# The order of work in the merges and at the output of a hybrid flow-matching step

## The chip, the cores and the metric

One core of one Trainium2 chip runs the kernel. The metric is the device time of one execution in microseconds. Five instruction streams matter: TensorE (PE, with its weight loads listed apart as PEld), VectorE (DVE), ScalarE (ACT), GpSimd (POOL) and SyncE (SP), which here only issues DMAs. Each stream runs in the order in which it was laid down; an instruction that waits holds up all that stands behind it on the same engine.

## The reference, cut to what matters

One layer of a hybrid backbone runs on 2048 noisy tokens ("sample") and 128 context tokens ("prompt"), with a model width of 1024. Three branches of width 512 are computed from the same projection: a bidirectional chunked gated-delta scan, a spatial-gating MLP and a Fourier mix. What this change touches is behind the branches:

```python
    br = jnp.stack([o_a, o_b, o_c], axis=2)
    pb = jnp.einsum('btnw,nwd->btnd', br, w_branch)
    gt = jax.nn.sigmoid(gates.reshape(B, T, N_BRANCH, D_MODEL))
    merged = jnp.einsum('btnd,btnd->btd', gt, pb)
    return jnp.einsum('btd,de->bte', merged, w_out), s_f, s_b
...
    h = h + gate[:, None, :] * out
    y_sample = rmsnorm(h, final_g)
```

`rmsnorm` divides a row by the root of its mean square (plus 1e-6) and multiplies by `final_g`. The prompt gets the same end with its own gate. All data are float32.

## The kernel before, in words

**Numbers.** A float32 matrix is held as two float16 parts, hi and lo, and a product is three matmuls: hi by hi, hi by lo, lo by hi. Before a weight block is split, its squares are summed on ScalarE (L309, into `wss`, then cast as `wscb`), a small matmul with ones on TensorE spreads the sum, VectorE makes a power of two from it (L271 to L273), and ScalarE and VectorE write hi and lo (L321, L322). `weight_step` advances this by one step at a time, between tiles of other work.

**Merges.** `merge(n, ...)` runs once for each branch, in the order 1 (MLP), 2 (Fourier), 0 (scan). For each of 8 column blocks `db` and each of 5 token tiles (four of 512, one of 128) there is a gate product of 24 matmuls on `xh`, `xl`, a sigmoid on ScalarE (L1717, remembered in `gated_[0]`), a branch product of 12 matmuls on `o16` (`big`), a product with the gate on VectorE (L1723 or L1726), and for the later branches an addition on POOL (L1727). `o16` is filled by `branch_block`: it loads a row of the branch's output (`st<-br`), converts it to hi on ScalarE (L1683) and to lo on VectorE (L1684). The first merge converts two tiles ahead of its first gate and the others as it goes; in its last block it converts the rows of the next merge behind each tile, and so does the second merge for the third. While the first two merges run, the steps of the scan are laid in between by a pace-maker (`pace`); `pace.drain()` in the last block of the second merge ends the scan.

**Order.** The planner of the kernel's framework lays the instructions of each engine into a queue with a timeline model, in order of readiness and of the program. Some edges are written by hand: `tc.issue_after(x)` puts the instructions of a block behind `x` on the same engine, and `tc.high_priority()` puts them forward. `behind_gate()` gives the weight squares (L308) and the row conversions (L1682) such an edge to the newest gate, once there is one. `_InTurn` wraps VectorE, ScalarE and TensorE: while `kept` is true, each instruction gets an edge to the one before it, so that the queue is the program's order.

**Output.** The output product is computed for pairs of 128-token tiles by `two_tiles`, with seven products of 12 matmuls instead of eight, on operands `pa` that the last merge has prepared as sums and differences. Eight pairs run in the order of `firsts` (8, 10, 12, 14, 0, 2, 4, 6); `tw[0]` to `tw[3]` are sums of the output weights that all pairs use. Between products VectorE sums PSUM banks with SBUF (`total`, L2008), POOL multiplies by the gate and adds the residual rows (`gated`, L2003, L2004), and `rows_done` squares a row (L1972), takes the root on POOL (L254), scales on VectorE (L1974, with `fg`, which is final_g) and stores it. The last pair (`end`) is written out by hand: `gate_add` (two VectorE operations), `piece` (a square on ScalarE, and a product with `fg` in place on POOL or VectorE), `summed_up`, the roots on POOL (L2053), the scaling on ScalarE (L2054). The prompt's left half is done before the pairs (`prompt_left`), its right half behind them (`prompt_right`).

**Loads of the output.** `in_turn` issues loads on SP in a fixed order from `ahead_out`'s gate on: the prompt's left rows, `pa` of the first pair, `tw[1]`, the rows of the first pair, `tw[2]`, `tw[0]`, `tw[3]`, `fg`, the prompt's right gate and rows (`gp_right`, `x_right`), `pa` of the second pair, the rows of the second pair, `pa` of the third. Later pairs are loaded one by one as buffers come free; `pa` has three places: in the room of `xl`, in `opa` and in `orp`. `gp_right` is used first on POOL behind the fourth pair (L2126).

Of the kernel before, what the change touches and what calls it, by code (L numbers as in the profile page):

```python
# [14 lines left out]
AF = mybir.ActivationFunctionType  # L15
ALU = mybir.AluOpType
# [4 lines left out]
P = 128  # L21
D = 1024
# [166 lines left out]
def hybrid_flow_kernel(ctx: ExitStack, tc: tile.TileContext, x_prompt, x_sample, state_delta, c, c_ctx, w_ada,  # L189
# [45 lines left out]
    mhalf = sb(cp, [P, 1], "mhalf")  # L235
    G.memset(mhalf, -0.5)

    newest, gated_ = [None], [None]

    def behind_gate():  # L240
        return tc.issue_after(gated_[0].ins) if gated_[0] is not None else ExitStack()

    def mm(out, l, r, start=True, stop=True, reopened=False):
        newest[0] = PE.matmul(out, l, r, start=start, stop=stop, skip_group_check=reopened)  # L244
# [1531 lines left out]
    def finish_delta(db):  # L1776
        if db == KT - 1:
            pace.drain()

    early = list(range(KT))  # L1780

# [211 lines left out]
    def two_tiles(t, pa, xr, hh, end):  # L1993


        pl = ps_d if odd_pair[0] else ps_mm
        odd_pair[0] ^= 1
        a, Y, X = [bank(pl, [P, 512]) for _ in range(3)]
        p1 = sb(ep, [P, 512], "sg", bufs=4)
        u2, u3 = [sb(ep, [P, 512], "st", bufs=3) for _ in range(2)]  # L2000

        def gated(j, cs):
            G.tensor_tensor(hh[j][:, cs], hh[j][:, cs], gb[:, cs], ALU.mult)  # L2003
            G.tensor_tensor(hh[j][:, cs], hh[j][:, cs], xr[j][:, cs], ALU.add)  # L2004

        def total(out, ps, other):
            with tc.high_priority():
                V.tensor_tensor(out, ps, other, ALU.add)  # L2008
# [12 lines left out]
        product(X, pa, 3, summed(0), True)  # L2021
        total(hh[1][:, right], X, u3)
        if not end:
            gated(1, right)
            product(Y, pa, 2, summed(3), False)
            total(hh[1][:, left], Y, p1)
            gated(1, left)
            product(X, pa, 6, quarter(4, 512), False)
            total(hh[0][:, right], X, u2)
            gated(0, right)  # L2030
            for j in (1, 0):
                rows_done(t + j, hh[j], xr[j])
            return
        total(u2, X, u2)
        gate_add(p1, p1, gb[:, left], xr[1][:, left])
        gate_add(hh[1][:, right], hh[1][:, right], gb[:, right], xr[1][:, right])
        piece(1, 0, xr[1], hh[1], right, G)
        gate_add(u2, u2, gb[:, right], xr[0][:, right])
        piece(0, 0, xr[0], hh[0], left, G)
        product(Y, pa, 2, summed(3), False)  # L2040
        with tc.high_priority():
            gate_add(hh[1][:, left], Y, gb[:, left], p1)
            piece(1, 1, xr[1], hh[1], left, V)
        Z = bank(ps_mm, [P, 512])
        product(Z, pa, 6, quarter(4, 512), True)
        with tc.high_priority():
            made = gate_add(hh[0][:, right], Z, gb[:, right], u2)
            piece(0, 1, xr[0], hh[0], right, V)
        with tc.issue_after(made.ins):
            for j, i in ((1, 0), (0, 0), (1, 1), (0, 1)):  # L2050
                summed_up(j, i)
        for j in (1, 0):
            G.tensor_tensor(norms[:, j:j + 1], parts[j][:, 1:2], mhalf, ALU.pow)  # L2053
            A.activation(hh[j], hh[j], AF.Copy, scale=norms[:, j:j + 1])  # L2054
            SY.dma_start(y_sample[0, (t + j) * P:(t + j + 1) * P], hh[j])

    parts = [sb(op, [P, 3], f"part{j}", bufs=1) for j in range(3)]
    norms = sb(op, [P, 3], "norms", bufs=1)

    def piece(j, i, junk, h, cs, on):  # L2060
        squared = A.activation(junk[:, cs], h[:, cs], AF.Square, accum_out=parts[j][:, i:i + 1])
        if on is not None:
            on.tensor_tensor(h[:, cs], h[:, cs], fg[:, cs], ALU.mult)
        return squared

    def summed_up(j, i):
        q_ = parts[j]
        if i:
            V.scalar_tensor_tensor(q_[:, i:i + 1], q_[:, i:i + 1], 1.0 / D, q_[:, i - 1:i], ALU.mult, ALU.add)
        else:  # L2070
            V.tensor_scalar(q_[:, 0:1], q_[:, 0:1], 1.0 / D, EPS, ALU.mult, ALU.add)

    def gate_add(out, src, gate, other):
        V.tensor_tensor(out, src, gate, ALU.mult)
        return V.tensor_tensor(out, out, other, ALU.add)

    def prompt_left():
        ps = bank(ps_mm, [P, 512])
# [4 lines left out]
        A.activation(gp[0], x_left, AF.Square, accum_out=parts[2][:, 0:1])  # L2083

    def prompt_right():
        after = None
        for i, cs in ((1, slice(0, 384)), (2, slice(384, 512))):
            ps = bank(ps_mm, [P, cs.stop - cs.start])
            gemm_N(ps, *p16, wo, 512 + cs.start, cs.stop - cs.start)
            with tc.high_priority(), tc.issue_after(after.ins) if i > 1 else ExitStack():  # L2090
                after = gate_add(gp_right[:, cs], ps, gp_right[:, cs], x_right[:, cs])
                A.activation(x_right[:, cs], gp_right[:, cs], AF.Square, accum_out=parts[2][:, i:i + 1])
                (G if i == 1 else V).tensor_tensor(gp_right[:, cs], gp_right[:, cs], fg[:, 512 + cs.start:512 + cs.stop], ALU.mult)
        with tc.issue_after(after.ins):
            for i in range(3):
                summed_up(2, i)
        n_ = norms[:, 2:3]
        G.tensor_tensor(n_, parts[2][:, 2:3], mhalf, ALU.pow)
        A.activation(x_left, x_left, AF.Copy, scale=n_)
        A.dma_start(y_prompt[0, :, left], x_left)  # L2100
        V.tensor_scalar(gp_right, gp_right, n_, None, ALU.mult)
        SY.dma_start(y_prompt[0, :, right], gp_right)

    in_turn(x_left, xp_[0:P, left])
# [52 lines left out]
```

## Time and profile before

| | us |
|---|---|
| median of 3 runs | 2162.39 |
| lowest and highest | 2161.81, 2163.25 |
| the profiled execution, its own time | 2166.18 |
| span of its profile, first to last instruction | 2164.4 |

The profile is that of one execution. A view by stretches gives, for each stretch of the span, how long each engine was busy with how many instructions, the clock that was granted to TensorE (1.00 is full) and the busy share of the DMA engines. A row of a timeline gives the start, the length, the engine, the line, the operation, the tiles written and read (buffer numbers left out), and in brackets how long the engine stood idle before it and what ended that. In a table of waits the numbers are the sum, the count and the longest. A line can be that of a helper: all matmuls are L244, so the tile names tell them apart (`wohi`, `wolo`: output weights; `pa`: operands of a pair; `tw`: sums of weights; `xl`: the room in which some of these lie). SPq and ACTq rows are DMAs at the moment of their issue.

The stretches: the first merge begins near 1030, the second near 1390, the third near 1735; the output begins near 1993 with the prompt's left half, the last matmul ends near 2155, and the span ends at 2164.4.

### The profile page before, as it was taken

What the parts mean: (1) busy time and instruction counts of PE and PEld (TensorE: products, weight loads), DVE (VectorE), ACT (ScalarE), POOL (GpSimd) and SP (SyncE); (2) the same over time, 40 slices, a digit from 0 to 9 for tenths busy, and PEclk for the clock granted to TensorE, in tenths of its full rate; (3) what the DMA queues carried; (4) which work ended last, traced back from release to release, by engine and by line L of the source; (5) the groups of instructions that cost most, each with busy time, mean ns of one, the idle gap of its engine ahead of it and who ended that gap; (6) DMA issues with size and microseconds to landing.
All of it is one profiled execution on the core that took longest, in us unless ns stands there. A gap on an engine that the chain in (4) does not pass through costs nothing.

```text
span 2164.4 us, 42587 instructions
## 1 busy us (share of the span) xinstructions
PE 2088.8 (97%) x16133; PEld 1197.1 (55%) x16133; DVE 1357.1 (63%) x3101; ACT 1061.7 (49%) x2457; POOL 751.7 (35%) x933
## 2 busy tenths in 40 slices
PE   7999999999999999999899999999999999999998
PEld 4455444455555677777455555566555444444444
DVE  6656754389878797466655546756555554666245
ACT  5554744476555664445544445656543343453112
POOL 0321332233333432443222233345443234334364
PEclk9999999999999999999899999999999999999999
DMA  9525732277776743444655555867664645456852
GB/s 350 218 77 195 258 114 89 82 230 218 247 228 218 236 147 93 125 146 120 224 175 168 162 172 166 269 211 213 191 189 135 204 167 177 166 196 241 329 204 103
DMA packets 222909, 403.24 MB, mean 186 GB/s; under 512 B 39720, under 2 KB 109632, under 8 KB 219888
## 3 DMA queue, kind: packets, MB, share of 16 engines
q1 hardware_dynamic: 167664, 290.84, 42.2%
q0 software_dynamic: 15216, 65.89, 8.0%
q10 hardware_dynamic: 39824, 43.79, 6.1%
q8 instruction: 127, 2.08, 0.4%
q14 instruction: 78, 0.64, 0.1%
HBM read 258.19 MB, written 142.24 MB: 185 GB/s over the span
## 4 chain that ended last, share of the span: by engine, by line
PE 47%; DMA 8%; DVE 5%; ACT 2%; issue 1%; POOL 1%; SPq 0%; POOLq 0%; DVEq 0%; ACTq 0%
PE b L244 47%; DMA st<-br 2%; DMA pa<-pa 1%; DMA ES<-ei 1%; DMA br<-o 1%; DMA xh<-in_x_sample_dram 1%; DMA ei<-XB 1%; DVE big L1684 1%; DMA mrg<-mrow 0%; DMA S<-in_state_delta_dram 0%; DMA skn<-kv 0%; ACT big L1683 0%; PE b L1373 0%; DMA sn<-n 0%; DVE sg L470 0%
## 5 line engine op out<-in xcount | busy, mean ns | idle before, releaser
L244 PE MATMUL b<-xh,whi 128*128 128x512 f16 (+1 forms) x1920 | 650.9, 348 | 4.7 <-DVE sg L1447 2.5
L244 PE MATMUL b<-xl,whi 128*128 128x512 f16 (+1 forms) x1920 | 651.2, 348 | 0.0
L244 PE MATMUL b<-xh,wlo 128*128 128x512 f16 (+1 forms) x1920 | 650.6, 348 | 0.0
L244 PEld LDWEIGHTS <-whi 128*128 128x128 f16 x3888 | 355.6, 98 | 328.4 <-issue 11.8
L244 PEld LDWEIGHTS <-wlo 128*128 128x128 f16 x1944 | 190.5, 98 | 175.4 <-issue 3.8
L244 PE MATMUL b<-big,bhi 128*128 128x512 f16 (+1 forms) x960 | 251.5, 348 | 3.9 <-ACT big L1683 3.2
L244 PE MATMUL b<-big,blo 128*128 128x512 f16 (+1 forms) x480 | 163.3, 347 | 0.0
L1727 POOL TENSOR_TENSOR mrow<-mrow,sg 128x512 f32<-128x512 f32 (+1 forms) x80 | 93.0, 1163 | 145.9 <-DVE sg L1726 105.2
L244 PEld LDWEIGHTS <-xh 128*128 128x128 f16 x1496 | 119.0, 99 | 31.7 <-issue 2.5
L244 PEld LDWEIGHTS <-bhi 128*128 128x128 f16 x960 | 86.9, 98 | 77.9 <-ACT big L1683 2.9
L947 POOL TENSOR_TENSOR cy<-cy,raw 128x545 f32<-128x545 f32 (+1 forms) x48 | 64.1, 1361 | 182.4 <-ACT raw L946 182.4
L244 PEld LDWEIGHTS <-xl 128*128 128x128 f16 x1068 | 99.0, 99 | 44.6 <-DMA tw<-tw 2.0
L1717 ACT ACTIVATE sg<-b,winv 128x512 f32<-128x512 f32 (+1 forms) x120 | 74.0, 617 | 95.4 <-PE b L244 94.8
L1181 POOL COPY T<-ES 32x256 f16<-32x256 f16 x68 | 30.6, 450 | 198.0 <-DMA ES<-ei 189.8
L244 PE MATMUL b<-whi,xh 128*128 128x128 f16 x544 | 95.4, 222 | 2.7 <-DVE yT L1633 2.0
L244 PE MATMUL b<-wlo,xh 128*128 128x128 f16 x544 | 95.4, 222 | 0.0
L244 PE MATMUL b<-whi,xl 128*128 128x128 f16 x544 | 95.4, 222 | 0.0
L322 DVE SCALAR_TENSOR_TENSOR wlo<-wst,wsc,whi 128x1024 f16<-128x1024 f32 x52 | 67.7, 1303 | 34.1 <-ACT whi L321 34.0
L321 ACT ACTIVATE whi<-wst,wsc 128x1024 f16<-128x1024 f32 x52 | 59.4, 1145 | 51.4 <-DVE wsc L272 49.5
L1726 DVE SCALAR_TENSOR_TENSOR sg<-b,binv,sg 128x512 f32<-128x512 f32 (+1 forms) x80 | 53.4, 669 | 36.4 <-PE b L244 33.2
L1288 POOL TENSOR_TENSOR skn<-skn,ed 128x512 f32<-128x512 f32 x34 | 38.0, 1116 | 109.6 <-DMA skn<-kv 104.5
L244 PEld LDWEIGHTS <-pa 128*128 128x128 f16 x420 | 41.4, 99 | 54.5 <-DMA pa<-pa 3.8
(526 smaller groups left out, 4313.6 us busy)
## 6 DMA issues: line engine op xcount, KB each, us to landing
wst<-in_w_blk_dram SPq DMA_DIRECT2D x58, 512.0 KB, 3.9
pa<-pa POOLq DMA_DIRECT2D x16, 896.0 KB, 4.6
qkv<-cy POOLq DMA_DIRECT2D x12, 1089.0 KB, 5.3
st<-br SPq DMA_DIRECT2D x48, 256.0 KB, 3.6
mrow<-mrg SPq DMA_DIRECT2D x16, 576.0 KB, 4.6
pa<-pa SPq DMA_DIRECT2D x5, 1792.0 KB, 8.6
dc<-dec SPq DMA_DIRECT2D x17, 512.0 KB, 4.7
kq<-qkv SPq DMA_DIRECT2D x34, 256.0 KB, 4.9
```

The source lines that it names most:

```text
L244: newest[0] = PE.matmul(out, l, r, start=start, stop=stop, skip_group_check=reopened)
L321: w.made = A.activation(w.hi, st, AF.Copy, scale=s)
L322: w.low = V.scalar_tensor_tensor(w.lo, st, s, w.hi, ALU.mult, ALU.subtract)
L947: G.tensor_tensor(y[:, c0:c1], y[:, c0:c1], raw[:, 1 + c0:1 + c1], ALU.mult)
L1181: G.tensor_copy(T16[rows(a0, b), :, :, b], ES[0:32, :, 2 * a0 + b, :, wT])
L1288: G.tensor_tensor(h3(kn_), h3(kn_), bc(ed[:, d, t, :], P), ALU.mult)
L1684: V.scalar_tensor_tensor(o16[:, 1, g, t0:t0 + tn], st, s, o16[:, 0, g, t0:t0 + tn], ALU.mult, ALU.subtract)
L1717: gated_[0] = A.activation(sg, ps, AF.Sigmoid, scale=gw.inv)
L1726: V.scalar_tensor_tensor(sg, ps, binv[:, 1:2], sg, ALU.mult, ALU.mult)
L1727: G.tensor_tensor(mr, mr, sg, ALU.add)
```

## The change

1. `behind_gate()` gives its edge only once `queued[0]` is set, which `finish_delta` does in the last block of the second merge. Weight squares and row conversions traced before that, in the first and second merge, have no edge to a gate; from there on they have it as before.
2. In the output's loads, `pa` of the second pair comes directly behind `tw[3]`, ahead of `fg`; `gp_right` and `x_right` come behind `pa` of the third pair.
3. From the last pair's X on, VectorE, ScalarE and TensorE keep the program's order, and that order is written anew: product Z is traced directly behind product Y; `u2`'s gate and residual go to POOL; the products with `fg` are apart from the squares, those of row 1 on POOL and those of row 0 on VectorE; sums and roots stand where their parts are ready; the prompt's right half follows in the same kept order, both its products with `fg` on VectorE.

```diff
-    newest, gated_ = [None], [None]
+    newest, gated_, queued = [None], [None], [False]
 
     def behind_gate():
-        return tc.issue_after(gated_[0].ins) if gated_[0] is not None else ExitStack()
+        return tc.issue_after(gated_[0].ins) if queued[0] else ExitStack()
...
     def finish_delta(db):
         if db == KT - 1:
             pace.drain()
+            queued[0] = True
...
+        in_order(True)
         total(u2, X, u2)
-        gate_add(p1, p1, gb[:, left], xr[1][:, left])
-        gate_add(hh[1][:, right], hh[1][:, right], gb[:, right], xr[1][:, right])
-        piece(1, 0, xr[1], hh[1], right, G)
-        gate_add(u2, u2, gb[:, right], xr[0][:, right])
-        piece(0, 0, xr[0], hh[0], left, G)
+        add_gated(u2, u2, gb[:, right], xr[0][:, right], G)
+        add_gated(p1, p1, gb[:, left], xr[1][:, left], V)
+        add_gated(hh[1][:, right], hh[1][:, right], gb[:, right], xr[1][:, right], V)
+        squared(1, 0, xr[1], hh[1], right)
+        squared(0, 0, xr[0], hh[0], left)
         product(Y, pa, 2, summed(3), False)
-        with tc.high_priority():
-            gate_add(hh[1][:, left], Y, gb[:, left], p1)
-            piece(1, 1, xr[1], hh[1], left, V)
         Z = bank(ps_mm, [P, 512])
         product(Z, pa, 6, quarter(4, 512), True)
-        with tc.high_priority():
-            made = gate_add(hh[0][:, right], Z, gb[:, right], u2)
-            piece(0, 1, xr[0], hh[0], right, V)
-        with tc.issue_after(made.ins):
-            for j, i in ((1, 0), (0, 0), (1, 1), (0, 1)):
-                summed_up(j, i)
+        final(hh[0], hh[0], left, left, V)
+        final(hh[1], hh[1], right, right, G)
+        summed_up(1, 0)
+        summed_up(0, 0)
+        add_gated(hh[1][:, left], Y, gb[:, left], p1, V)
+        squared(1, 1, xr[1], hh[1], left)
+        final(hh[1], hh[1], left, left, G)
+        add_gated(hh[0][:, right], Z, gb[:, right], u2, V)
+        squared(0, 1, xr[0], hh[0], right)
+        summed_up(1, 1)
+        root(1, 1)
+        final(hh[0], hh[0], right, right, V)
+        summed_up(0, 1)
+        root(0, 1)
         for j in (1, 0):
-            G.tensor_tensor(norms[:, j:j + 1], parts[j][:, 1:2], mhalf, ALU.pow)
             A.activation(hh[j], hh[j], AF.Copy, scale=norms[:, j:j + 1])
             SY.dma_start(y_sample[0, (t + j) * P:(t + j + 1) * P], hh[j])
 
+    def in_order(kept):
+        V.kept = A.kept = PE.kept = kept
...
+    def squared(j, i, junk, h, cs):
+        A.activation(junk[:, cs], h[:, cs], AF.Square, accum_out=parts[j][:, i:i + 1])
+
+    def final(out, h, cs, fs, on):
+        on.tensor_tensor(out[:, cs], h[:, cs], fg[:, fs], ALU.mult)
...
+    def root(j, i):
+        G.tensor_tensor(norms[:, j:j + 1], parts[j][:, i:i + 1], mhalf, ALU.pow)
+
+    def add_gated(out, src, gate, other, on):
+        on.tensor_tensor(out, src, gate, ALU.mult)
+        on.tensor_tensor(out, out, other, ALU.add)
...
     def prompt_right():
-        after = None
-        for i, cs in ((1, slice(0, 384)), (2, slice(384, 512))):
+        cols = slice(0, 384), slice(384, 512)
+        summed_up(2, 0)
+        for i, cs in enumerate(cols):
             ps = bank(ps_mm, [P, cs.stop - cs.start])
             gemm_N(ps, *p16, wo, 512 + cs.start, cs.stop - cs.start)
...
+            add_gated(gp_right[:, cs], ps, gp_right[:, cs], x_right[:, cs], V)
+            squared(2, 1 + i, x_right, gp_right, cs)
+        final(gp_right, gp_right, cols[0], slice(512, 896), V)
+        summed_up(2, 1)
+        summed_up(2, 2)
+        root(2, 2)
+        final(gp_right, gp_right, cols[1], slice(896, D), V)
+        A.activation(x_left, x_left, AF.Copy, scale=norms[:, 2:3])
...
     sums_of(3)
+    next_pair(in_turn)
     in_turn(fg, final_g[None, :].to_broadcast([P, D]))
-    in_turn(gp_right, gateD[1:2, right].to_broadcast([P, 512]))
-    in_turn(x_right, xp_[0:P, right])
-    next_pair(in_turn)
...
         if i == 0:
             next_pair(in_turn)
+            in_turn(gp_right, gateD[1:2, right].to_broadcast([P, 512]))
+            in_turn(x_right, xp_[0:P, right])
```

More of the change, by code (lines that the diff above doesn't have):

```diff
@@ L2058, in hybrid_flow_kernel @@
     norms = sb(op, [P, 3], "norms", bufs=1)
[L2060 to L2064, printed above, removed]
+    def squared(j, i, junk, h, cs):
+        A.activation(junk[:, cs], h[:, cs], AF.Square, accum_out=parts[j][:, i:i + 1])
+    def final(out, h, cs, fs, on):
+        on.tensor_tensor(out[:, cs], h[:, cs], fg[:, fs], ALU.mult)
@@ L2071, in summed_up @@
             V.tensor_scalar(q_[:, 0:1], q_[:, 0:1], 1.0 / D, EPS, ALU.mult, ALU.add)
-    def gate_add(out, src, gate, other):
-        V.tensor_tensor(out, src, gate, ALU.mult)
-        return V.tensor_tensor(out, out, other, ALU.add)
+    def root(j, i):
[3 more added lines that the diff above has]
+        on.tensor_tensor(out, out, other, ALU.add)
     def prompt_left():
@@ L2085, in prompt_right @@
     def prompt_right():
-        after = None
-        for i, cs in ((1, slice(0, 384)), (2, slice(384, 512))):
+        cols = slice(0, 384), slice(384, 512)
+        summed_up(2, 0)
+        for i, cs in enumerate(cols):
             ps = bank(ps_mm, [P, cs.stop - cs.start])
             gemm_N(ps, *p16, wo, 512 + cs.start, cs.stop - cs.start)
[L2090 to L2099, printed above, removed]
+            add_gated(gp_right[:, cs], ps, gp_right[:, cs], x_right[:, cs], V)
[6 more added lines that the diff above has]
+        A.activation(x_left, x_left, AF.Copy, scale=norms[:, 2:3])
         A.dma_start(y_prompt[0, :, left], x_left)
-        V.tensor_scalar(gp_right, gp_right, n_, None, ALU.mult)
+        V.tensor_scalar(gp_right, gp_right, norms[:, 2:3], None, ALU.mult)
         SY.dma_start(y_prompt[0, :, right], gp_right)
```

## The prediction

> **What bounds the kernel now.** I read the page first, then busy time stretch by stretch, then TensorE's waits, and last the timelines of the few places where it stops.
>
> ```profile
> span 2164.4 us, 42587 instructions
> ...
> PE 2088.8 (97%) x16133; PEld 1197.1 (55%) x16133; DVE 1357.1 (63%) x3101; ACT 1061.7 (49%) x2457; POOL 751.7 (35%) x933
> ```
>
> TensorE is busy 97% of the span, so an edit off its path pays only where TensorE stands still, runs at a lower clock, or has finished. The busy time by stretch (columns: PE, PEld, DVE, ACT, POOL busy, granted clock, DMA share, GB/s) shows where that is:
>
> ```profile
> 1030.00:1040.00 10.00, 7.70 (x92) 6.12 (x90) 7.99 (x25) 7.83 (x19) 5.20 (x7) 0.78 0.88 289
> 1040.00:1050.00 10.00, 7.21 (x29) 2.93 (x28) 3.49 (x9) 4.69 (x11) 1.81 (x3) 0.53 0.71 228
> ...
> 2018.10:2025.70 7.60, 4.27 (x13) 1.58 (x13) 3.48 (x5) 2.30 (x4) 4.42 (x5) 0.78 1.02 416
> 2025.70:2139.70 114.00, 114.00 (x530) 51.69 (x529) 42.17 (x58) 16.65 (x29) 61.41 (x54) 1.00 0.53 195
> 2139.70:2155.30 15.60, 15.60 (x97) 8.32 (x95) 14.78 (x26) 4.24 (x11) 7.22 (x7) 1.00 0.17 68
> 2155.30:2164.40 9.10, 0.14 (x3) 0.00 (x0) 2.44 (x8) 3.29 (x7) 1.61 (x3) 0.68 0.44 173
> ```
>
> Three places touch this change: the merges (TensorE idle, low clock at their start), one hole in the output stage near 2018, and 9.1 us after the last matmul. Between 2025.7 and 2139.7 TensorE has no gap, so what is saved at 2018 reaches the end whole. In the last 15.6 us VectorE is busy 14.78: it, not TensorE, sets the tail.
>
> **The loads of the output.** The hole is one load, operands pa of the second pair of tiles:
>
> ```profile
> 2021.43 0.39 PE L244 MATMUL b<-wohi,pa 128*128 128x512 f16 x1 [3.33 <-DMA pa<-pa]
> ...
> 2025.72 2.75 PE L244 MATMUL b<-xl,pa 128*128 128x512 f16 x12
> ...
> 2028.31 1.89 PE L244 MATMUL b<-tw,pa 128*128 128x512 f16 x8
> ```
>
> TensorE waits 3.33 us, and pays again: the twelve matmuls of the product that starts at 2021.43 take 4.29 us to the next product, whose twelve take 2.59. The clock (0.78 in that stretch) costs 1.70 more. Why the load is late stands in the queue that issues it:
>
> ```profile
> 1993.44 0.80 SPq L1948 DMA_DIRECT2D tw<-tw  x2
> 1994.29 0.48 SPq L1948 DMA_DIRECT2D fg<-in_final_g_dram  x1
> 1995.47 0.32 SPq L1948 DMA_DIRECT2D xl<-gate  x1
> 1999.24 0.33 SPq L1948 DMA_DIRECT2D xl<-in_x_prompt_dram  x1
> 2001.98 0.37 SPq L1948 DMA_DIRECT2D pa<-pa  x1
> ...
> 2025.93 0.38 SPq L1948 DMA_DIRECT2D pa<-pa  x1
> ```
>
> Behind the sums (tw) come fg, the prompt's gate (gp_right, here xl<-gate) and rows (x_right), then pa. Here are size and time from issue to landing, then the DMA share around 2036:
>
> ```profile
> tw<-tw SPq DMA_DIRECT2D x2, 1024.0 KB, 18.9
> fg<-in_final_g_dram SPq DMA_DIRECT2D x1, 512.0 KB, 19.6
> ...
> 2034.00:2036.00 2.00, 2.00 (x11) 0.89 (x10) 0.00 (x0) 0.00 (x0) 0.86 (x1) 1.00 1.00 392
> 2036.00:2038.00 2.00, 2.00 (x11) 0.87 (x9) 1.38 (x2) 0.00 (x0) 0.37 (x1) 1.00 0.16 63
> ```
>
> The engines are full; loads land in the order of issue: tw at 1993.44 + 18.9 = 2012.3, fg at 1994.29 + 19.6 = 2013.9, 0.52 MB in 1.6 us. The change puts pa (1792 KB, 1.84 MB) in fg's place. At the 416 GB/s of the stretch above it takes 4.4 us and lands at 2012.3 + 4.4 = 2016.7, perhaps 2017.1. TensorE asks for it at 2021.43 - 3.33 = 2018.1. So **the wait goes: -3.33, and with it the slow product: -1.70**. Bounds: all of it, or, if landing is not strictly in order, only what the overtaken 1.05 MB (2.5 us) bring, 0.8 us of wait left.
>
> What is late next? The third pair's pa is issued at 2025.93 and nothing but it can be the last to land when the DMA falls silent, 0.16 of 2 us into the last row, 2036.3. The pair of TensorE that needs it would now start at 2018.1 + 7 products x 2.59 = 2036.2. But gp_right and x_right (256 KB each) move behind it: 0.52 MB, 1.3 us, so 2035.0. Spare 1.2 us: cost 0; without that cover 0.1 us. fg now lands near 2018.4, and VectorE asks for it at 2022.1:
>
> ```profile
> L1974 DVE SCALAR_TENSOR_TENSOR xh<-xh,hss,fg x8: 1277/1284/2281, 2022.1 to 2089.1; 128x1024 f32<-128x1024 f32 x8
> ```
>
> Cost 0, with 3.7 us of cover; if it were later, VectorE's next PSUM sums would queue behind it. gp_right and x_right are first touched on POOL after the fourth pair, so their move costs 0. No DMA is added.
>
> **The merges.** No instruction is added or taken away; some 30 weight squares (L309) and 32 row conversions (L1683: 12 of the first merge's rows, 20 of the second's) lose the edge that held them behind a gate on ScalarE. The gain can only be TensorE's waits that hang on them:
>
> ```profile
> PE b L1373 <- ACT o L1369: 4.4, 3, 2.7
> PE b L244 <- ACT o L1234: 4.4, 3, 2.7
> ...
> PE b L244 <- ACT big L1683: 3.2, 2, 2.8
> PE b L244 <- DVE wscb L258: 2.5, 2, 1.3
> ...
> 1391.74 0.16 PE L244 MATMUL b<-wscb,ones 128*128 128x1 bf16 x1 [1.21 <-DVE wscb L258]
> 1396.36 0.22 PE L244 MATMUL b<-u,kn 128*128 128x128 f16 x1 [0.63 <-ACT u L1224]
> 1397.97 0.78 PE L244 MATMUL b<-u,kn 128*128 128x128 f16 x11 [0.96 <-DVE u L1225]
> ```
>
> Only wscb (2.5 us, twice) waits directly for a square. The first of the two, 1.3, stands just ahead of the 2.8 us for converted rows (big), whose first two blocks no gate holds back before either; TensorE would reach that wait sooner and gain 0. The second, 1.21 at 1391.74, is followed by 0.63 and 0.96 for the scan's u, which can take it back. I take half: **-0.6**, from 0 to -1.2 by these rows. Indirectly ScalarE, freer of squares at the wrong moment, could shorten the scan's 4.4 + 4.4: at best -8.8 more.
>
> The loss: a square or conversion that the planner now puts ahead of a gate waits there for its DMA, and the gates and the scan's ScalarE steps (u, o, kn, R) queue behind it. ScalarE already does this:
>
> ```profile
> ACT big L1683 <- DMA st<-br: 40.9, 26, 3.5
> ```
>
> 26 waits, 40.9 us, while TensorE's waits for ScalarE in the merges are 4.4 + 4.4 + 3.2. I put this at 0, since most of those 40.9 us cost TensorE nothing, and keep +12.0 (these waits doubled) as the bound.
>
> **The end.** The new order is kept on VectorE, ScalarE and TensorE. The rows with which I walk it (first the times, then mean ns of one by shape):
>
> ```profile
> 2146.55 0.68 DVE L2008 TENSOR_TENSOR xh<-b,st 128x512 f32<-128x512 f32 x1
> ...
> 2150.15 1.28 DVE L2074 TENSOR_TENSOR xh<-b,wst 128x512 f32<-128x512 f32 x2
> ...
> 2159.53 0.72 ACT L2099 ACTIVATE xh<-xh,norms 128x512 f32<-128x512 f32 x1 [1.65 <-POOL norms L2098]
> 2160.28 0.38 ACTq L2100 DMA_DIRECT2D out_dram<-xh  x1
> ...
> L2063 POOL TENSOR_TENSOR xh<-xh,fg 128x512 f32<-128x512 f32 x2 | 2.9, 1438 | 6.2 <-ACT xh L2061 6.2
> L2098 POOL TENSOR_TENSOR norms<-part,mhalf 128x1 f32<-128x1 f32 x1 | 0.5, 548 | 0.3 <-DVE part L2069 0.3
> ...
> L2074 DVE TENSOR_TENSOR sg<-sg,wst 128x512 f32<-128x512 f32 x1 | 1.0, 984 | 0.0
> ...
> L2061 ACT ACTIVATE xh<-xh 128x512 f32<-128x512 f32 x4 | 2.5, 622 | 9.1 <-DVE xh L2075 9.1
> L2054 ACT ACTIVATE xh<-xh,norms 128x1024 f32<-128x1024 f32 x2 | 2.2, 1140 | 1.2 <-POOL norms L2053 1.2
> ```
>
> Between 2146.55 and 2150.15 lie six VectorE operations, 0.60 each. Saved on VectorE: u2's two (1.2) go to POOL, one final product changes places with another. Lost: p1's two, done before in a pause (the 984 ns row is the first), now come after X's sums: +1.2. And final(hh[0], left) is in place, so VectorE waits for both squares. In the clock of the trace before: X's sums, p1 and hh[1] right end near 2150.3; two squares (0.62 each) until 2151.6; one product and two small sums, 2152.4; Y's and Z's four operations, 2154.8. ScalarE squares Y's at 2153.6 to 2154.2, POOL multiplies until 2155.6 and only then takes root(1,1), 0.55: 2156.2. Scaling the two rows (1.14 each) holds ScalarE until 2158.4, then come the prompt's squares (384 and 128 columns, 0.8 by the 0.62 for 512), VectorE's product and sums (0.8), root (0.55), scaling (0.72): ScalarE's DMA goes out at 2161.3 instead of 2160.28, **+1.0**. The prompt's stores are as large as before, so the rest of the end keeps its length. Bounds: the last L1974 (1.28) slipping into the new wait, -0.3; four POOL operations that each cost VectorE 0.30, as the 984 ns row against the 0.68 of one alone, +2.2. TensorE's order (Y, then Z) costs 0: the same 24 matmuls, under VectorE's work.
>
> Beside that 0.30 stands a rule that speaks against the change. The Trainium skill (SBUF — State Buffer, Who interferes with whom) says that a VectorE instruction with two SBUF inputs and a GpSimd one that reads SBUF exclude each other for a whole instruction. By that, four POOL operations of 1.3 would block up to 5.2 us instead of 1.2; the 984 ns row shows 0.30 for one, so the sum goes by the row.
>
> **Sum**, against the profiled execution's own 2166.18 us (span 2164.4 and 1.8 around it; the median of the runs, 2162.39, lies 3.8 below): -3.33 - 1.70 - 0.6 + 1.0 = -4.6, so 2161.6 for that execution and **2157.8** for the median.
>
> **The rivals.**
> 1. The wait for pa moves instead of going: it lands a little late, or the third pair's does. For it: spare is only about 1 us in both places. Against it: tw, fg in strict order. Half of 3.33 and the clock loss kept: +1.7 + 1.7, 2161.2.
> 2. Slower: ScalarE stands at late rows and weights in the two merges, gates and scan behind it. Price: 4.4 + 4.4 + 3.2 = 12.0 more, 2157.8 + 12.0 = 2169.8. It decides from 4.6 us of added TensorE idle, and passes 0.2% at 8.9. For it: 26 such waits already, and the low clock at 1030 to 1050, which makes idle dearer. Against it: TensorE waits for conversions only twice.
> 3. The scan gains: ScalarE's 8.8 us for o and o's norm shrink by two thirds, -6: 2151.8.
> 4. POOL and VectorE exclude each other for whole operations in the tail: 4 x (1.3 - 0.3) = 4.0 more, 2161.8.
> 5. The planner puts squares and rows where they were: the -0.6 is lost, 2158.4, inside the forecast, with 0.08 of its chance.
>
> **How the numbers follow.** Forecast (5 within it) 0.48, its own range 2154 to 2162; 0.2% (4.3 us), about what can be told from no change, cuts it at 2158.1: 0.32 faster, 0.16 same. Rival 1: 0.09 (0.02 faster, 0.07 same). Rival 2: 0.24 (0.22 slower, 0.02 same). Rival 3: 0.15, all faster. Rival 4: 0.04, same. Faster 0.49, same 0.29, slower 0.22. The range runs from forecast less 8.8 (2149) to rival 2's 2170.
>
> **What would show it.** pa of the second pair issued right behind tw near 1994, no TensorE wait there, clock 1.00 through that pair; no new wait at the third. No 1.21 for wscb; ScalarE's waits before L1683 not above 40.9 us. From the last matmul to the last DMA about 1 us more than before. I am wrong if idle in the merges grows by more than 4 us, or if the tail grows by more than 2.2.

## The result, and the profile after

| | median, us (runs) | kernel before beside it, us (runs) | ratio, 95% interval |
|---|---|---|---|
| the changed kernel | 2157.78 (20) | 2162.89 (20) | 0.9974 [0.9966, 0.9982] |

The change makes the kernel faster by 0.26%, 5.1 us by the medians, 5.6 us (3.9 to 7.4) by the ratio. Single runs lie between 2154.08 and 2163.91, those of the kernel before between 2158.84 and 2170.13. The profiled execution took 2157.86 us itself, span 2156.0.

The head of the page of the changed kernel:

```profile
span 2156.0 us, 42627 instructions
...
PE 2082.2 (97%) x16133; PEld 1195.7 (55%) x16133; DVE 1360.5 (63%) x3100; ACT 1060.6 (49%) x2457; POOL 758.3 (35%) x934
```

TensorE does the same 16133 matmuls in 6.6 us less busy time. Below are its stretches (columns as before): the one in which the second pair begins (2011.33), which held the hole in the kernel before, the 114 us from that pair's second product on, and the tail from the last matmul to the end of the span.

```profile
2008.00:2015.60 7.60, 7.60 (x37) 3.42 (x35) 1.66 (x4) 2.38 (x4) 7.21 (x7) 1.00 1.01 383
2013.90:2127.90 114.00, 114.00 (x530) 51.63 (x529) 44.69 (x61) 17.80 (x31) 63.52 (x57) 1.00 0.57 210
...
2143.65:2156.00 12.35, 0.00 (x0) 0.00 (x0) 5.82 (x15) 4.85 (x11) 3.68 (x4) 0.62 0.33 128
```

Behind one wait for `tw` (1.6 us, 1.0 before) the output runs without a gap at full clock; the tail is 12.35 us, against 9.1 before. The queue of SP in the changed kernel, and all waits of TensorE in its output (sum, count, longest):

```profile
1986.41 0.85 SPq L1949 DMA_DIRECT2D tw<-tw  x2
1987.31 0.45 SPq L1949 DMA_DIRECT2D pa<-pa  x1
1988.13 3.63 SPq L1949 DMA_DIRECT2D fg<-in_final_g_dram  x1
...
2017.31 0.38 SPq L1949 DMA_DIRECT2D pa<-pa  x1
2017.74 0.68 SPq L1949 DMA_DIRECT2D xl<-gate  x1
2018.47 0.50 SPq L1949 DMA_DIRECT2D xl<-in_x_prompt_dram  x1
```

```profile
PE b L244 <- DMA tw<-tw: 1.6, 1, 1.6
```

`pa` of the second pair goes out behind `tw`, and TensorE waits for no `pa` any more, neither for the second pair's nor for the third's.

For the merges, two lines serve as a clock of their own: the 120 gates (L1717) and the 128 operations by which the scan writes its output (L1234). The view of one line gives count, shortest, median and longest, and the start of the first and the last. First the kernel before, then the changed one:

```profile
L1717 ACT ACTIVATE sg<-b,winv x120: 344/684/690, 1032.5 to 1991.5; 128x512 f32<-128x512 f32 x96, 128x128 f32<-128x128 f32 x24
...
L1234 ACT ACTIVATE o<-b,eg x128: 348/368/405, 937.7 to 1664.9; 128x128 f32<-128x128 f32 x128
```

```profile
L1717 ACT ACTIVATE sg<-b,winv x120: 342/670/702, 1040.5 to 1984.2; 128x512 f32<-128x512 f32 x96, 128x128 f32<-128x128 f32 x24
...
L1234 ACT ACTIVATE o<-b,eg x128: 348/367/402, 943.0 to 1649.6; 128x128 f32<-128x128 f32 x128
```

From the first gate to the last it is 959.0 us before and 943.7 after, and the scan's last output comes 632.4 us behind the first gate before, 609.1 after. But this clock starts late in the changed kernel, because its first gate is itself held up. ScalarE stands 3.06 us there at a weight square which the planner now lays ahead of that gate, the scan's `S` waits behind it, and TensorE waits for `S`:

```profile
1039.39 0.63 ACT L309 ACTIVATE blo<-wst 128x512 f16<-128x512 f32 x1 [3.06 <-DMA wst<-in_w_brb_dram]
...
1040.68 0.24 PE L244 MATMUL b<-S,sk 128*128 128x128 f16 x1 [2.30 <-ACT S L1224]
```

In the kernel before TensorE waits 1.28 us near this place, for `wscb`. A fairer start is the first matmul on `S` and `sq` just ahead of the wait: in both kernels 8216 matmuls stand before it. It starts at 1032.62 before and at 1037.80 after, and from there to the last gate it is 958.9 and 946.4 us. So the merges still got shorter by far more than the 0.6 us of the forecast. How much of it is the change, and not the one execution, is for the experiments.

The tail of the changed kernel, where the kept order shows as L182: the last matmul, VectorE's operations that ran beside POOL's, those of POOL, and ScalarE's last step.

```profile
2143.43 0.22 PE L182 MATMUL b<-wohi,wlo 128*128 128x128 f16 x1
...
2134.47 0.68 DVE L182 TENSOR_TENSOR sg<-sg,wst 128x512 f32<-128x512 f32 x1
2135.18 1.64 DVE L182 TENSOR_TENSOR sg<-sg,xh 128x512 f32<-128x512 f32 x1
2136.74 1.75 DVE L182 TENSOR_TENSOR xh<-xh,wst 128x512 f32<-128x512 f32 x1
2138.53 0.69 DVE L182 TENSOR_TENSOR xh<-xh 128x512 f32<-128x512 f32 x1
2140.62 1.25 DVE L182 TENSOR_TENSOR xh<-xh,fg 128x512 f32<-128x512 f32 x1 [1.40 <-ACT xh L182]
...
2144.63 1.22 DVE L182 SCALAR_TENSOR_TENSOR part<-part 128x1 f32<-128x1 f32 x1
...
2134.63 1.65 POOL L2086 TENSOR_TENSOR st<-st,wst 128x512 f32<-128x512 f32 x1 [2.72 <-DVE st L182]
2136.35 1.59 POOL L2087 TENSOR_TENSOR st<-st,xh 128x512 f32<-128x512 f32 x1
2140.05 1.27 POOL L2073 TENSOR_TENSOR xh<-xh,fg 128x512 f32<-128x512 f32 x1 [2.11 <-ACT xh L182]
2144.15 1.68 POOL L2073 TENSOR_TENSOR xh<-xh,fg 128x512 f32<-128x512 f32 x1 [2.83 <-ACT xh L182]
...
2146.89 2.19 ACT L182 ACTIVATE xh<-xh,norms 128x1024 f32<-128x1024 f32 x2 [1.43 <-POOL norms L2083]
...
2151.92 0.38 ACTq L182 DMA_DIRECT2D out_dram<-xh  x1
```

From the start of the last matmul to ScalarE's last DMA it is 2151.92 - 2143.43 = 8.49 us, against 2160.28 - 2155.22 = 5.06 before: the end is 3.43 us longer. And VectorE stands still beside POOL: an operation of 0.68 us takes 1.64 and 1.75, one of 128x1, else 0.15, takes 1.22. Each is done 0.54 or 0.55 us after POOL's operation (2134.63 + 1.65 = 2136.28, and 2136.82; 2137.94 and 2138.49; 2141.32 and 2141.87); the small one 0.02 after. That is VectorE's own work laid behind the whole of POOL's. POOL's operations too take up to 1.68 instead of 1.27 when VectorE was first.

### The profile page after: what moved, and what is told of

Its sections match the earlier page's. It is cut to its first block, busy times and chain, and to the rows that moved or that the text cites. A ratio compares the mean times of both kernels' runs of the same rounds, so it can differ in the third digit from the quotient of the medians.

```text
span 2156.0 us, 42627 instructions
## 1 busy us (share of the span) xinstructions
PE 2082.2 (97%) x16133; PEld 1195.7 (55%) x16133; DVE 1360.5 (63%) x3100; ACT 1060.6 (49%) x2457; POOL 758.3 (35%) x934
## 4 chain that ended last, share of the span: by engine, by line
PE 52%; DVE 9%; DMA 5%; ACT 3%; issue 2%; POOL 1%; SPq 0%; ACTq 0%; POOLq 0%; DVEq 0%
PE b L244 51%; DMA st<-br 2%; DVE XB L1107 1%; DVE E L1108 1%; DMA ei<-XB 1%; DMA tw<-tw 1%; DMA br<-o 0%; DMA XB<-nd 0%; DVE sg L1447 0%; DVE big L1684 0%; DMA N<-n 0%; ACT big L1683 0%; DVE XB L1116 0%; DVE n L1077 0%; DMA S<-in_state_delta_dram 0%
## 5 line engine op out<-in xcount | busy, mean ns | idle before, releaser
L244 PEld LDWEIGHTS <-whi 128*128 128x128 f16 x3856 | 351.1, 98 | 324.3 <-issue 10.4
L1717 ACT ACTIVATE sg<-b,winv 128x512 f32<-128x512 f32 (+1 forms) x120 | 73.9, 616 | 92.8 <-PE b L244 92.2
L309 ACT ACTIVATE wlo<-wst 128x1024 f16<-128x1024 f32 x52 | 54.9, 1056 | 52.1 <-DMA wst<-in_w_blk_dram 47.2
```

Source lines behind the costliest of these rows:

```text
L309: w.squared = A.activation(w.lo, st, AF.Square, accum_out=ss)
L1717: gated_[0] = A.activation(sg, ps, AF.Sigmoid, scale=gw.inv)
```

## The experiments

**The three parts alone, and two of them together.** `gates` is part 1 of the change, `loads` part 2, `end` part 3, `gates_loads` parts 1 and 2 with the old end. The edits are those of the diff above; their cores:

```diff
# gates
-        return tc.issue_after(gated_[0].ins) if gated_[0] is not None else ExitStack()
+        return tc.issue_after(gated_[0].ins) if queued[0] else ExitStack()
# loads
+    next_pair(in_turn)
     in_turn(fg, final_g[None, :].to_broadcast([P, D]))
-    in_turn(gp_right, gateD[1:2, right].to_broadcast([P, 512]))
-    in_turn(x_right, xp_[0:P, right])
-    next_pair(in_turn)
# end
+        in_order(True)
         total(u2, X, u2)
-        gate_add(p1, p1, gb[:, left], xr[1][:, left])
...
+        add_gated(u2, u2, gb[:, right], xr[0][:, right], G)
```

Expected of `loads`:

> Only the output's loads are reordered. Theory of the prediction: the 3.33 us wait for pa and the 1.70 us of slow clock behind it go, nothing else moves: 5.0 us faster than before, ratio 0.9977, and from the first matmul of the prompt's left half to the last matmul about 157.4 us (162.2 before). Rival, that the wait moves to the third pair: 1 to 2 us faster, with a new wait near the start of that pair.

Expected of `gates`:

> Only the edges to gates are taken away in the first two merges. Theory of the prediction: 0.6 us faster, 0 to 1.2, the waits for wscb (2.5 us) gone and nothing else. Rival, read from the two profiles side by side: TensorE's waits in the two merges fall from 23 us to about 16, the time by 3 to 7 us, most of it in waits for the scan's last steps (o, oss) that no square stands in front of. Third reading: no gain at all, the difference of the profiles being that of two executions; then ratio 1.000.

Expected of `end`:

> Only the end is reordered. Theory of the prediction: 1.0 us slower, from the last matmul to the last DMA issued by ScalarE 5.8 us (4.84 before), VectorE losing 0.30 us for each of four POOL operations beside it. Rival, that VectorE and POOL exclude each other for whole operations: 8.3 us from the last matmul to that DMA, 3.4 us slower than before, ratio 1.0016, with VectorE additions of 1.6 us where POOL adds beside them.

Expected of `gates_loads`:

> The change without its new end. If the end costs 3.4 us: 2154.4 us by the median, ratio 0.9961, faster than both kernels, with 4.84 us from the last matmul to the last DMA issued by ScalarE. If the end costs 1.0 us: 2156.8, ratio 0.9972. If the end were neutral or a gain: 2157.8 or above.

| | median, us (runs) | ratio to before (2163.01, 31 runs) | in us, by the ratio |
|---|---|---|---|
| `loads` | 2159.26 (12) | 0.9982 [0.9968, 0.9996] | -3.9 (-0.9 to -6.9) |
| `gates` | 2157.97 (12) | 0.9983 [0.9967, 0.9999] | -3.7 (-0.2 to -7.1) |
| `end` | 2165.90 (12) | 1.0013 [1.0001, 1.0026] | +2.8 (+0.2 to +5.6) |
| `gates_loads` | 2154.27 (8) | 0.9955 [0.9939, 0.9971] | -9.7 (-6.3 to -13.2) |

The three add up to -4.8, near the -5.6 of the whole: as far as the intervals tell, none hides another. The end loses, by the 3.4 us of its rival rather than by the 1.0 of the prediction's theory. The two other parts without it are faster than the kernel before, and by the medians faster than the changed kernel too (2154.27, where 2154.4 was expected for an end that costs 3.4), though those two intervals just touch. `loads` did what its theory says: from the start of the prompt's first output matmul to that of the last matmul it is 156.92 us, against 161.98 before, 5.06 less. `gates` gained more than the 0.6 of the theory. Start of the last matmul to ScalarE's last DMA is 5.05 us in `loads` and `gates`, 8.50 in `end`, as exactly as one execution can show it. In `gates` the hole of the output is there as it was, slow clock and all:

```profile
2012.40 0.39 PE L244 MATMUL b<-wohi,pa 128*128 128x512 f16 x1 [3.08 <-DMA pa<-pa]
...
2009.00:2016.60 7.60, 4.52 (x14) 1.59 (x13) 3.48 (x5) 2.30 (x4) 4.74 (x5) 0.78 1.03 417
```

**Which half of the gates' part, and the kernel before once more.** `behind_any` is the old `behind_gate`. `squares_free` uses it for the row conversions, so that only the weight squares are free in the first two merges; `rows_free` uses it for the squares, so that only the conversions are free. `before_again` is the kernel before, unchanged, for a second profile of it.

```diff
# squares_free
-            with behind_gate():
+            with behind_any():
                 A.activation(o16[:, 0, g, t0:t0 + tn], st, AF.Copy, scale=s)
# rows_free
-        with behind_gate():
+        with behind_any():
             w.squared = A.activation(w.lo, st, AF.Square, accum_out=ss)
```

> The kernel before once more, for a second profile of it. If the profile of before was one long execution by chance: from the first gate to the last 945 to 950 us. If the merges' gain of some 10 us seen in the profiles is the kernel's: 953 to 959 us again, with the fourth of the eight scan-end waits (o, oss) back near 1540 to 1620.

> Weight squares free of the gates in the first two merges, row conversions still behind them. If the squares carry the gain: some 4 us faster than before and 945 us from the first gate to the last, wscb waits of TensorE gone. If the rows carry it: 0, and 953 to 959 us.

> Row conversions free of the gates in the first two merges, squares still behind them. If the rows carry the gain: some 4 us faster and 945 us from the first gate to the last; if the squares do: 0, 953 to 959 us, and TensorE's waits for wscb (2.5 us) still there. If any change of ScalarE's order shifts the scan, both halves gain something.

`before_again` took 2163.37 us (one run); `squares_free` has a median of 2157.41 (10 runs), ratio 0.9963 [0.9944, 0.9982]; `rows_free` 2158.76 (10), 0.9980 [0.9963, 0.9997], beside 2162.59 (29) of the kernel before. Either half gains by itself, and as far as the intervals tell the gains do not add: both together (`gates`, 0.9983) are no more than the rows alone. That is what the last line of the expectation of `rows_free` says. First to last gate is 951.9 in `before_again`, just between its two expected ranges, 940.0 in `squares_free` and 946.0 in `rows_free`. The first gate is held up in `squares_free` as in the changed kernel, but not in `rows_free`; from the matmul on `S` and `sq` the three take 951.8, 942.7 and 945.9. TensorE's waits for `wscb` are gone in `squares_free`, and one of them (1.3 us) is left in `rows_free`.

**First or second merge.** `squares_first` frees the squares in the first merge only (the edge is back from the second on), `squares_second` in the second only; the row conversions keep their edge in both. One run each.

```diff
# squares_first
+    queued[0] = True
     inv_ = merge(2, False, inv_, finish_delta, then=(0, 17), step=norm_step)
# squares_second (queued starts as True)
+    queued[0] = False
     inv_ = merge(2, False, inv_, finish_delta, then=(0, 17), step=norm_step)
```

> Only the squares of the first merge go without their gates; nothing else is changed. The gain of the gates' part lies in the stretch from the 61st to the 71st gate (second half of the second merge): about 94 us with the gates, 84.6 us without. If the second merge's own squares (or its rows) shift the scan, this stretch stays at about 94 us and first to last gate at 952 to 959 us. If the freedom in the first merge is passed on through ScalarE's order, the stretch is 84 to 87 us and first to last gate 940 to 946 us.

> Only the squares of the second merge go without their gates. If the gain arises in the second merge: the stretch from the 61st to the 71st gate is 84 to 87 us and first to last gate 940 to 946 us. If it arises in the first: about 94 us, and 952 to 959 us.

`squares_first` took 2156.64 us, `squares_second` 2161.16. The gates and the scan's outputs, first of `before_again`, then of these two (lines there are 3 higher):

```profile
L1717 ACT ACTIVATE sg<-b,winv x120: 342/687/688, 1036.4 to 1988.3; 128x512 f32<-128x512 f32 x96, 128x128 f32<-128x128 f32 x24
...
L1234 ACT ACTIVATE o<-b,eg x128: 349/367/403, 940.2 to 1663.1; 128x128 f32<-128x128 f32 x128
```

```profile
L1720 ACT ACTIVATE sg<-b,winv x120: 343/670/705, 1040.8 to 1981.2; 128x512 f32<-128x512 f32 x96, 128x128 f32<-128x128 f32 x24
...
L1237 ACT ACTIVATE o<-b,eg x128: 351/368/408, 941.5 to 1644.6; 128x128 f32<-128x128 f32 x128
```

```profile
L1720 ACT ACTIVATE sg<-b,winv x120: 343/679/705, 1039.1 to 1988.3; 128x512 f32<-128x512 f32 x96, 128x128 f32<-128x128 f32 x24
...
L1237 ACT ACTIVATE o<-b,eg x128: 348/368/407, 941.5 to 1660.7; 128x128 f32<-128x128 f32 x128
```

The scan's last output comes 626.7 us behind the first gate in `before_again` (1663.1 - 1036.4), 603.8 with the squares of the first merge free, 621.6 with those of the second. First to last gate is 951.9, 940.4 and 949.2; from the matmul on `S` and `sq` it is 951.8, 943.1 and 949.0. So in these single executions the freedom of the first merge's squares already gives the whole gain. That of the second's fits neither line of its expectation: it shortens its own stretch from the 61st to the 71st gate (87.2 us against 93.7), but brings only 2.7 us from the first gate to the last. The stretches of the second merge show where the gain of `squares_first` lies: columns as before, from the 41st to the 61st gate and from there to the 71st, `before_again` first, then `squares_first`.

```profile
1393.51:1564.63 171.12, 167.06 (x1506) 100.03 (x1504) 105.38 (x269) 100.83 (x289) 85.40 (x109) 1.00 0.67 210
1564.63:1658.36 93.73, 88.56 (x719) 51.44 (x717) 54.12 (x137) 43.67 (x127) 37.14 (x39) 0.98 0.55 175
```

```profile
1396.96:1568.44 171.48, 170.00 (x1554) 103.10 (x1552) 110.08 (x277) 101.53 (x298) 88.30 (x114) 1.00 0.72 219
1568.44:1652.20 83.76, 83.76 (x693) 48.74 (x690) 52.86 (x131) 42.29 (x122) 34.11 (x34) 1.00 0.58 184
```

In the same 171 us TensorE does 48 matmuls more, and stands still 1.5 us instead of 4.1; then it has 26 fewer to do and no gap, where it had 5.2 us of gaps and a lower clock. The scan is laid one step earlier: of its 32 groups of outputs, 23 are done by the 51st gate in the four kernels with the edges (`before`, `before_again`, `loads`, `end`) and in `squares_second`, 24 in the nine others, in which the squares or the rows of the first merge are free. In these kernels the earlier step and the gain go together; that the step is the cause is argued from this, and `squares_second`, with a shorter stretch and no earlier step, shows that it is not the only thing at work.

**The end: who holds VectorE.** `u2_vector` is the changed kernel with `u2`'s two operations back on VectorE; `pool_roots_only` moves both products with `fg` of row 1 there too, so that POOL has only the roots.

```diff
# both
-        add_gated(u2, u2, gb[:, right], xr[0][:, right], G)
+        add_gated(u2, u2, gb[:, right], xr[0][:, right], V)
# pool_roots_only
-        final(hh[1], hh[1], right, right, G)
+        final(hh[1], hh[1], right, right, V)
...
-        final(hh[1], hh[1], left, left, G)
+        final(hh[1], hh[1], left, left, V)
```

> The changed kernel with u2's gate and residual on VectorE again, in the same place, so that POOL is free there. If POOL and VectorE exclude each other: VectorE's two additions of 1.64 and 1.75 us fall to 0.68, two operations of 0.60 are added, 0.8 us gained or more: 7.4 us from the last matmul to the last DMA issued by ScalarE (8.28 in the changed kernel). If they only slow each other by 0.30: 0.6 us lost, 8.9 us.

> The new end with the u2 operation and both last multiplications of the second row block on VectorE, so that GpSimd has the roots alone there. If VectorE stands still while a GpSimd operation on two inputs runs: VectorE's operations are back at 0.6 to 0.7 us and at 0.15 us for the small one, and the start of the last matmul to ScalarE's last DMA falls to about 7.3 us (8.49 in the changed kernel, 7.89 with u2 alone moved). If only the amount of work on VectorE counts: two operations of 0.60 us more on it, 8.3 us or more.

`u2_vector`: 2157.46 us (12 runs), 0.9976 [0.9957, 0.9995], not to be told from the changed kernel by the times. In its trace the operations of VectorE beside `u2` are back at 0.69 us, and last matmul to last DMA is 7.89: 0.60 less, though VectorE has two operations more. That fits the exclusion (-0.8 or more), if a little short of it, and not the 0.30 of the prediction (+0.6). POOL still has the two products with `fg`, and beside them VectorE still takes 1.25 us for a product and 1.23 for a small sum.

`pool_roots_only` took 2154.23 us (one run), and its tail is 8.39. Its VectorE, with the last matmul, in the part that matters:

```profile
2139.96 0.22 PE L182 MATMUL b<-wohi,wlo 128*128 128x128 f16 x1
...
2136.60 1.29 DVE L182 TENSOR_TENSOR xh<-xh,fg 128x512 f32<-128x512 f32 x2 [1.40 <-ACT xh L182]
...
2140.13 0.69 DVE L182 TENSOR_TENSOR xh<-xh,fg 128x512 f32<-128x512 f32 x1 [0.79 <-ACT xh L182]
2140.74 0.68 DVE L182 TENSOR_TENSOR xh<-b,wst 128x512 f32<-128x512 f32 x1
2141.46 0.69 DVE L182 TENSOR_TENSOR xh<-xh,st 128x512 f32<-128x512 f32 x1
2142.07 0.15 DVE L182 SCALAR_TENSOR_TENSOR part<-part 128x1 f32<-128x1 f32 x1
2142.94 0.69 DVE L182 TENSOR_TENSOR xh<-xh,fg 128x512 f32<-128x512 f32 x1 [0.72 <-ACT xh L182]
...
2148.35 0.38 ACTq L182 DMA_DIRECT2D out_dram<-xh  x1
```

One half of the expectation came true: no operation is stretched (0.69, and 0.15 for the small one). The 7.3 us did not. The product of row 1 now stands in the kept order ahead of Z's two operations and waits 0.79 us for the square on ScalarE, and the last product waits 0.72 more. I had counted the work that moves to VectorE and not what it waits for there. (The 1.40 us ahead of the first product stand in the changed kernel as well, and the walk of the prediction had them.) The rival's "8.3 or more" is met in size, but not for its reason, since the added work alone is 2 x 0.60 while 1.51 us are waits.

**The best of the parts.** `squares_loads` has free squares, gated rows, the new order of the loads and the old end.

> The weight squares of the first two merges go without their gates, the row conversions keep theirs, the output's loads are in the new order, its end in the old one. If the squares alone carry the gain in the scan: about -5 to -8 us for them and -3.9 to -5 us for the loads, 2150 to 2154 us, ratio 0.994 to 0.996, and about 5.05 us from the start of the last matmul to ScalarE's last DMA, as in the kernel before. If the rows' freedom is worth something of its own beside the squares', it is slower than 'gates_loads' (2154.3 us); if the rows' freedom costs (they come early and stand in ScalarE's way), it is faster.

It took 2148.22 us (6 runs, beside 2164.25 of the kernel before in 11): 0.9932 [0.9909, 0.9956], 14.7 us (9.5 to 19.7) less by the ratio, the fastest kernel of all and below the 2150 to 2154 that were expected. It is faster than `gates_loads` (0.9955 [0.9939, 0.9971]) as `squares_free` is faster than `gates`, 0.2% both times, and its first to last gate is 941.0 us against 943.9. But the intervals overlap in both pairs: that the rows' freedom costs something beside the squares' is likely and not settled.

## Why the prediction was right, and where it was wrong

The forecast of 2157.8 was met by the median to 0.1 us, and it was right in kind. But its four terms, -3.33 - 1.70 - 0.6 + 1.0, were right in the first two only. The third was 3 to 5 us too small a gain by the times, the fourth some 2 us too small a loss, and these errors took each other out: that the median was hit so closely is luck. One of the prediction's own signs of being wrong came true: the tail was to grow by no more than 2.2 us, and it grew by 3.4.

**The loads: right.** -5.03 was worked out; the hole and the slow product are gone, and `loads` alone gives -3.9 (-0.9 to -6.9) by the times and -5.06 in its trace. The product that took 4.29 us starts at 2011.33 and the next at 2013.92 in the changed kernel, 2.59 as forecast. Nothing is late next: no wait at the third pair, none for `fg`. So landing in the order of issue, which the sum took from `tw` and `fg`, fits here too, and rival 1 did not come. In the profile of `loads`, 0.32 us of wait for `pa` is left, so the margin, about 1 us in the sum, can be used up.

**The merges: mis-sized, -0.6 against some -4 to -6.** `gates` alone gives -3.7 (-0.2 to -7.1), and `gates_loads` lies 5.8 below `loads`. The profiles give more: four kernels with the edges took a mean of 954.5 us from first to last gate (959.0, 951.9, 954.0, 953.0), four with both freedoms 944.5 (945.7, 943.9, 943.7, 944.8), 10.0 less. Of this, 2.8 us are only the late first gate: from the matmul on `S` and `sq` the means are 954.4 and 947.2, 7.2 less. TensorE stands still 3.1 us less (16.6 against 19.7), and the same matmuls keep it busy 4.1 us less (930.6 against 934.7), since the granted clock there is 1.00 instead of 0.99. The sum of the prediction counted idle time alone in the merges, though it counted the clock at the hole. And the first four executions were on average 3.3 us above their kernels' medians, the others (`gates`, `gates_loads`, the changed kernel, `u2_vector`) 0.8 below; if all of these 4.2 us arose in the merges, 3.0 are left. So the traces do not fix the size better than the times do. The step that failed is "the gain can only be TensorE's waits that hang on them". I looked for waits on squares and conversions and found `wscb`. That wait is gone, yet most of the gain goes with the order: with the squares or the rows freed the planner lays a step of the scan earlier. My "indirectly ScalarE could shorten the scan's 4.4 + 4.4" (rival 3, -6, given 0.15) was the right kind, and its rows, waits for `o`, did shrink, from 4.4 + 4.4 (4.2 + 2.1 in `before_again`) to 2.5 + 0.2. These are the waits of TensorE in the merges of the changed kernel:

```profile
PE b L244 <- ACT S L1224: 2.9, 2, 2.3
PE b L244 <- ACT o L1234: 2.5, 2, 1.3
PE b L244 <- ACT big L1683: 1.9, 1, 1.9
...
PE b L1373 <- ACT o L1369: 0.2, 1, 0.2
```

Which of the planner's choices in the first merge moves the scan's step in the second is open.

**Rival 2: the waits came, and a small part of the price.** ScalarE does stand at weights now, as it did not before, and less at rows; these are its waits in the merges of the changed kernel.

```profile
ACT big L1683 <- DMA st<-br: 32.0, 22, 4.0
...
ACT wlo L309 <- DMA wst<-in_w_blk_dram: 21.2, 13, 3.5
ACT blo L309 <- DMA wst<-in_w_brb_dram: 3.1, 1, 3.1
```

These are 56.3 us together against 40.9, and TensorE's idle time from the matmul on `S` and `sq` to the last gate still fell, from 22.3 us to 16.0. The 12 us of the bound asked that what ScalarE loses reaches TensorE; ScalarE is busy 49% and has the room. In one place it does reach TensorE, and the prediction put that at 0: at the last of these rows, the square ahead of the first gate, TensorE waits the 2.3 us for `S` shown above, where it waited 1.28 us before. All seven kernels of the experiments in which the first merge's squares are free have this wait (2.2 to 2.4 us), and `rows_free` does not. A kernel that keeps only this square behind the gate was not tried.

**The end: mis-sized, +1.0 against +3.4.** By times +2.8 (0.2 to 5.6), in the traces 3.4 in each of two. The walk beside what was measured, both in the clock of the kernel before (the changed kernel's times plus 11.79, those of `pool_roots_only` plus 15.26, so that the last matmuls agree):

| step | predicted | changed kernel | POOL with roots only |
|---|---|---|---|
| X's sum, p1 and hh[1] right done | 2150.3 | 2151.0 | 2150.5 |
| Y's and Z's four operations done | 2154.8 | 2156.5 | 2157.4 |
| two rows scaled | 2158.4 | 2160.9 | 2160.8 |
| ScalarE's DMA | 2161.3 | 2163.7 | 2163.6 |

With POOL away the first line of the walk comes out, but by two errors that cancel: VectorE does two operations more there, and X's sums begin 1.5 us earlier than the walk had them (2145.05 against 2146.55). In the kernel before, `p1`'s two operations did not fill a pause, as the walk has it: VectorE works without a break from 2143.01 to 2146.55, and these two stand among what holds X's sums back. Moved behind them, they let the sums begin earlier, and this takes back part of the loss. With POOL beside it VectorE loses 0.96 + 1.07 us in two operations (against 0.68 each), later 0.57 and 1.07: 3.67 in all, of which the sum had nothing and its bound 4 x 0.30. These 3.67 less the 1.5 are near the 2.4 us by which ScalarE's DMA goes out later than in the walk. The step that failed is the reading of one row. Here is the row of the 984 ns in the kernel before, with what POOL did beside it:

```profile
2143.72 0.98 DVE L2074 TENSOR_TENSOR sg<-sg,wst 128x512 f32<-128x512 f32 x1
...
2142.56 1.60 POOL L2063 TENSOR_TENSOR xh<-xh,fg 128x512 f32<-128x512 f32 x1 [0.85 <-ACT xh L2061]
```

POOL's operation ended at 2144.16, and VectorE's 0.54 later, at 2144.70. POOL's operation had only 0.44 us left when VectorE's came at 2143.72; the 0.30 was the price of that rest, not of a whole one. Rival 4 (they exclude each other for whole operations, given 0.04) was the right mechanism; its 4.0 for the blocking stands beside 3.67. By the rule of the Trainium skill (SBUF — State Buffer, Who interferes with whom) that was weighed there, the trace agrees, with 1.64 and 1.75 us.

The blocking is not the whole of the end's loss, though. Without any of it the tail is 8.39: once the products are on VectorE, the kept order makes it wait for ScalarE's squares. In the kernel before VectorE does Z's operations and the sums first and has no such wait until 2157.6. An order that takes both away was not tried.

## What to carry to other kernels

When a row shows an operation stretched beside another engine's, look at how the two overlap before taking the difference as the price of one: it may be only the rest of an operation that was nearly done. An ordering edge that stands on no wait of the bounding engine can still cost, because the planner lays other work around it; such an edit is sized by trying it, and both signs belong in the range. And try the parts of a change alone: here two gained, one lost, and the best kernel leaves the third out. A clock laid into a trace must start at an event that the change cannot move: the first gate came late by the change itself, and the gain looked 2.8 us larger than it was.

## What the runs showed of the hardware

- A VectorE operation on 128x512 with two SBUF operands that starts while POOL works on two SBUF operands ends about 0.55 us after POOL's whole operation, however early it started: 1.64 and 1.75 us for 0.68. An operation on 128x1 is held as well, 1.22 us for 0.15, and POOL itself takes 1.59 to 1.68 us for 1.27 when VectorE was first. VectorE operations that read one operand from PSUM were not held: in the kernel before, two of them take 1.28 us together from 2150.15 on, beside a POOL product of 1.28 us that starts at 2150.47.
- With one wait of 3.08 us in `gates`, the granted clock of the 7.6 us around it is 0.78, the same as with 3.33 us in the kernel before; where the wait is gone (changed kernel) the same products run at 1.00.
- Executions of one kernel on one core spread over 10 us and more (2158.84 to 2170.13, 20 runs of the kernel before), so a difference of a few us between single profiles, such as the 7.2 us of the merges, says little of its size without the medians.
